# Weights prepared two chunks at a time, a bias table laid out in memory, and the product A12 B21 at the end of the last step: a neighbourhood-attention layer on one core

## The chip, the core and the metric

The kernel runs on one core of a Trainium2 chip. The metric is the device time of one execution in microseconds (us); of several runs the median is given. The engines are named as in the profile: PE (matrix products), DVE (vector), ACT (scalar), POOL (GpSimd), SP (issues DMAs).

## What is computed

One layer of the encoder, in float32, for x of 512 tokens (8 rows by 64 columns) by 2048:

```python
h = rms_norm(x, norm_pre)
q, k, v, z = jnp.split(h @ w_in, 4, axis=-1)            # w_in 2048 x 8192, 16 heads of 128
# one_row(r), for every row r of the grid; with 8 rows all 8 are keys, and 16 columns about the query's
s = jnp.einsum('bqhd,bxqyhd->bhqxy', q_r, k_nb) * scale
s = s + rpb[:, dr[None, :, None], dc[:, None, :]]
p = jax.nn.softmax(s over the 128 neighbours)
o = jnp.einsum('bhqxy,bxqyhd->bqhd', p, v_nb)
y = (o * jax.nn.silu(z)) @ w_out                        # w_out 2048 x 2048
return x + rms_norm(y, norm_post)
```

## The kernel before

**Products.** The big products go through PE in the format fp32r. Each operand is split into a high part `hi` (a cast on ACT) and the rest `lo` (a subtraction on DVE), and a product is hi·hi + lo·hi + hi·lo, three matmuls. Their results are accumulated in PSUM.

**Steps.** Work runs in ten steps over the columns of W, of 1024 columns each. Steps 0 to 7 multiply with W_in and give q, k, v, z of two heads each; steps 8 and 9 multiply with W_out. Steps 0 and 8 are plain: 32 chunks of 12 matmuls with 512 columns. The others use seven products in place of eight (Strassen's scheme in Winograd's form), of block sums of A (the activations: A11, S1, A12, N2, A22, N4, N3) and of B (the weights: B11, B12, B21, B22 and running sums of them): seven passes of 8 chunks, 6 matmuls a chunk. A *chunk* is 128 rows of W by 512 columns (256 KB). The passes accumulate in the chains X, Y, X, Y, Z, Y, Z of two PSUM banks each; `combine` takes a chain apart after each pass. m numbers all chunks in order: step 3 is m = 144 to 199, its pass 2 is 160 to 167, its pass 3 is 168 to 175.

**A chunk's way.** `load_raw` (L205) brings a raw chunk through SP's queue into one of four buffers (`NRAW`), `load_t` (L122) a chunk of B11 or B12 into one of eight tiles T. `prep(m)` (L216) runs two chunks (`AHEAD`) ahead of the matmuls of m: in passes 1, 3 and 4 it adds raw to T on DVE (L223), casts hi on ACT (L231) and subtracts lo on DVE (L232), each with three buffers; in pass 5 it adds raw to T after the split (L239). Then it issues the loads that became possible.

**Attention beside it.** Beside step s the attention of two heads of step s - 1 is computed, by the table `HEAD`: at a chunk number, for instance, transposes on PE (tk, tq, tz, L393; the copies k5h, k5l, q5h, q5l of head 5 are their split, L398 to L407), the scores (L457), the bias added with the row maximum (L470), exponentials, the transposition and split of p (pt, L504 and L405), the product with v (o, L527) and the gate (zm, L533). The PSUM buffers of tag T are two, so tz takes that of tk. The bias of a head comes as a padded table of 184 KB into `braw` (POOL's queue, L434); three operations on DVE reverse it and add a mask (L440).

**The last step.** In step 9, pass 6 is cut in halves of 128 tokens each (`products` with one half, L287): all chunks of half 0, then `combine_last(0)`, all of half 1, then `combine_last(1)`. `finish(n, t, ...)` squares a block of columns n for tokens t, sums, computes the factor rcy by a power on POOL (L657), and multiplies by the weights of the norm (L658). `final(t)` scales, adds the residual xres in four parts (three on DVE, L668, one on ACT and POOL, L665 and L666) and writes to memory. `load_res` (L672) brings xres from the middle of pass 4 on; `final(0)` and `final(1)` stand in pass 6.

**What sets the order.** Instructions are written in the order of the loop at the end, and the tile scheduler moves them within each engine, except those issued through `InOrder`. An engine takes its instructions strictly in the order that results, and waits for semaphores at the head of its queue.

Of the kernel before, what the change touches and what calls it, by code (L numbers as in the profile page):

```python
# [38 lines left out]

NSTEP = HEADS // 2  # L40
# [9 lines left out]
NRAW = 4  # L50
# [15 lines left out]
def na_block(ctx: ExitStack, tc: tile.TileContext, xT, x, gpre, gpost, w, rpb, mask, out):  # L66
# [29 lines left out]
    mhalf = cp.tile([P, 4], F32, name="mhalf")  # L96
    nc.gpsimd.memset(mhalf, -0.5)
    mask_sb = cp.tile([P, 3, 32], F32, name="mask_sb")
# [21 lines left out]
    T = [cp.tile([P, L], F32, name=f"t{k}") for k in range(KH)]  # L120

    def load_t(step, q, k):  # L122
        nc.sync.dma_start(T[k], w[step, q, k])

# [61 lines left out]
    def where(m):  # L186
# [5 lines left out]
        return step, *divmod(m, KT if step in PLAIN else KH)  # L192
# [12 lines left out]
    def load_raw(m):  # L205
        raws[m] = wp.tile([P, L], F32, tag="raw", name=f"raw{m}", bufs=NRAW)
        step, p, k = where(m)
        if step in PLAIN:
            src = w[step, (B11, B12, B21, B22)[p + 2 * (k // KH)], k % KH]
        else:  # L210
            src = w[step, (None, B12, B21, B22, B21, B22)[p], k]
        nc.sync.dma_start(raws[m], src)
# [3 lines left out]
    def prep(m):  # L216
        step, p, k = where(m)
        plain = step in PLAIN
        if step == 0 and p == 0:
            take_x(k)  # L220
        src = raws.pop(m) if is_raw(m) else T[k]
        if not plain and p in (1, 3, 4):
            nc.vector.tensor_tensor(T[k], T[k], src, ALU.add)  # L223
# [7 lines left out]
        nc.scalar.copy(hi, src)  # L231
        nc.vector.tensor_tensor(lo, src, hi.bitcast(F32), ALU.subtract)  # L232
# [5 lines left out]
        elif p == 5:  # L238
            nc.vector.tensor_tensor(T[k], T[k], src, ALU.add)  # L239
# [6 lines left out]
    U, C = {}, {}  # L246
# [33 lines left out]
    def mm_seven(m):  # L280
        step, p, k = where(m)
        c = chain(p)
        if p in (0, 1, 4) and k == 0:
            b = (step + (c == "Y")) % 2
            U[c] = [pm.tile([P, L], F32, tag=f"u{2 * b + s}", name=f"u{step}{c}{s}") for s in range(2)]
        if step == LAST and p == 6:
            products(m, (0,))  # L287
            if k == KH - 1:
                combine_last(0)
                for mm in range(m - KH + 1, m + 1):  # L290
                    products(mm, (1,))
                combine_last(1)
# [24 lines left out]
    def combine(step, p):  # L317
        u = U[chain(p)]
        c = C.setdefault(step, {})
        if p == 0:  # L320
            c["12"] = pair(f"s1_{step}")
            for s in range(2):
                nc.scalar.copy(c["12"][:, s, :], u[s])
        elif p == 1:
            c["21"] = pair(f"s5_{step}")
            for s in range(2):
                nc.scalar.copy(c["21"][:, s, :], u[s])
        elif p == 2:
            c["11"] = pair(f"c11_{step}")
            for s in range(2):  # L330
                if step == LAST:
                    finish(2, s, u[s], c["11"][:, s, :])
                else:
                    nc.scalar.activation(c["11"][:, s, :], u[s], AF.Copy, scale=rc[:, s : s + 1])
        elif p == 3:
            c["22"] = pair(f"e_{step}")
            for s in range(2):
                nc.vector.tensor_tensor(c["22"][:, s, :], u[s], c["12"][:, s, :], ALU.subtract)
            nc.vector.tensor_tensor(c["21"], c["22"], c["21"], ALU.subtract)
# [413 lines left out]
```

## Time and profile before

| | before |
|---|---|
| median of 3 runs | 910.19 us (908.84 to 910.43) |
| the profiled execution | 909.24 us, of which the span is 907.5 |
| granted PE clock, mean | 0.992 |
| DMA | 163.32 MB, mean 180 GB/s |
| ACT cast hi from T, 128x512 | 312 times, 618 ns |
| DVE bias and mask, 128x256 | 48 times, 603 ns |

The span is the stretch that the profile records. A row of the groups names line, engine, operation, tiles and shapes; behind the bar stand the busy time, the mean duration and the idle time of the engine just before, with what ended it. A window's row gives for each engine the busy time and (x) the instructions, then the granted PE clock (1.00 is full), the busy share of the DMA engines, and GB/s. Timeline rows begin with start and duration; an operation's duration can overlap its successor's on the same engine, so the distance between two starts is what one costs in a full queue.

### The profile page before, as it was taken

What the parts mean: (1) busy time and instruction counts of PE and PEld (TensorE: products, weight loads), DVE (VectorE), ACT (ScalarE), POOL (GpSimd) and SP (SyncE); (2) the same over time, 40 slices, a digit from 0 to 9 for tenths busy, and PEclk for the clock granted to TensorE, in tenths of its full rate; (3) what the DMA queues carried; (4) which work ended last, traced back from release to release, by engine and by line L of the source; (5) the groups of instructions that cost most, each with busy time, mean ns of one, the idle gap of its engine ahead of it and who ended that gap; (6) DMA issues with size and microseconds to landing.
All of it is one profiled execution on the core that took longest, in us unless ns stands there. A gap on an engine that the chain in (4) does not pass through costs nothing.

```text
span 907.5 us, 13123 instructions
## 1 busy us (share of the span) xinstructions
PE 879.1 (97%) x4184; PEld 729.6 (80%) x4184; DVE 756.4 (83%) x1395; ACT 563.0 (62%) x1077; POOL 36.2 (4%) x63
## 2 busy tenths in 40 slices
PE   9999999999999999999999999999999999999981
PEld 7888888888888888888888888888878888888660
DVE  4477979897988998799879987989799756886877
ACT  6666857585658566755776576758576654455342
POOL 1000000000000000000000000000002000000003
PEclk9999999999999999999999999999999999999996
DMA  8894367637664765476546745773676334544795
GB/s 258 247 266 129 94 183 220 194 101 217 211 173 114 232 203 165 123 233 199 148 148 214 223 140 159 219 209 116 185 255 192 106 117 127 153 137 147 237 219 185
DMA packets 85877, 163.32 MB, mean 180 GB/s; under 512 B 10016, under 2 KB 10016, under 8 KB 85808
## 3 DMA queue, kind: packets, MB, share of 16 engines
q1 hardware_dynamic: 82080, 151.56, 55.8%
q0 software_dynamic: 3296, 10.41, 4.4%
q8 instruction: 32, 0.52, 0.2%
q10 hardware_dynamic: 432, 0.53, 0.2%
q14 instruction: 37, 0.30, 0.1%
HBM read 154.59 MB, written 7.86 MB: 179 GB/s over the span
## 4 chain that ended last, share of the span: by engine, by line
PE 85%; issue 5%; DMA 4%; DVE 3%; POOL 1%; ACT 1%; SPq 0%; DVEq 0%; POOLq 0%; ACTq 0%
PE u L269 19%; PE u1Y L308 4%; PE u4Y L308 4%; PE u5Y L308 4%; PE u6Y L308 4%; PE u3Y L308 4%; PE u2Y L308 4%; DMA raw<-in_w 3%; PE u1X L308 2%; PE u4X L308 2%; PE u3X L308 2%; PE u2X L308 2%; PE u7X L308 2%; PE u5X L308 2%; PE u6X L308 2%
## 5 line engine op out<-in xcount | busy, mean ns | idle before, releaser
L231 ACT CAST hi<-t 128x512 fp32r<-128x512 f32 x312 | 192.0, 618 | 134.4 <-DVE lo L232 26.0
L232 DVE TENSOR_TENSOR lo<-t,hi 128x512 fp32r<-128x512 f32 x312 | 212.8, 688 | 29.8 <-ACT hi L231 29.0
L232 DVE TENSOR_TENSOR lo<-raw,hi 128x512 fp32r<-128x512 f32 x192 | 131.7, 690 | 66.0 <-ACT hi L231 53.2
L231 ACT CAST hi<-raw 128x512 fp32r<-128x512 f32 x192 | 118.7, 620 | 103.9 <-DVE lo L232 23.5
L223 DVE TENSOR_TENSOR t<-t,raw 128x512 f32<-128x512 f32 x192 | 128.4, 688 | 6.3 <-DMA raw<-in_w 5.7
L269 PE MATMUL u<-hi,a 128*128 128x512 f32 x512 | 131.1, 392 | 1.4 <-ACT a L145 0.8
L269 PEld LDWEIGHTS u<-hi,a 128*128 128x128 f32 x512 | 95.0, 188 | 21.5 <-ACT a L145 1.3
L269 PE MATMUL u<-lo,a 128*128 128x512 f32 x256 | 70.8, 390 | 0.0
L269 PEld LDWEIGHTS u<-lo,a 128*128 128x128 f32 x256 | 48.1, 188 | 10.1
L239 DVE TENSOR_TENSOR t<-t,raw 128x512 f32<-128x512 f32 x64 | 42.9, 689 | 7.7 <-DMA raw<-in_w 7.7
L308 PE MATMUL u9Y<-hi,a 128*128 128x512 f32 x96 | 27.0, 398 | 3.6 <-ACT hi L231 3.6
L440 DVE TENSOR_TENSOR bm<-braw,mask_sb 128x256 f32<-128x256 f32 x48 | 27.5, 603 | 0.0
L308 PE MATMUL u1Y<-hi,a 128*128 128x512 f32 x96 | 26.8, 396 | 0.0
L308 PE MATMUL u4Y<-hi,a 128*128 128x512 f32 x96 | 26.8, 396 | 0.0
L308 PE MATMUL u5Y<-hi,a 128*128 128x512 f32 x96 | 26.8, 396 | 0.0
L308 PE MATMUL u3Y<-hi,a 128*128 128x512 f32 x96 | 26.8, 396 | 0.0
L308 PE MATMUL u6Y<-hi,a 128*128 128x512 f32 x96 | 26.8, 396 | 0.0
L308 PE MATMUL u2Y<-hi,a 128*128 128x512 f32 x96 | 26.8, 396 | 0.0
L308 PE MATMUL u7Y<-hi,a 128*128 128x512 f32 x96 | 26.8, 396 | 0.0
L146 DVE TENSOR_TENSOR a<-x,a 128x512 fp32r<-128x512 f32 x16 | 11.0, 690 | 18.2 <-ACT a L145 18.2
L434 POOL DMA_DIRECT2D braw<-in_rpb x16 | 8.6, 535 | 436.1 <-DVE bm L440 252.0
L308 PEld LDWEIGHTS u9Y<-hi,a 128*128 128x128 f32 x96 | 17.6, 188 | 9.2 <-ACT hi L231 5.9
(444 smaller groups left out, 1958.0 us busy)
## 6 DMA issues: line engine op xcount, KB each, us to landing
raw<-in_w SPq DMA_DIRECT2D x384, 256.0 KB, 2.9
t<-in_w SPq DMA_DIRECT2D x128, 256.0 KB, 2.9
x<-in_xT SPq DMA_DIRECT2D x16, 256.0 KB, 5.5
xres<-in_x SPq DMA_DIRECT2D x16, 256.0 KB, 8.2
graw<-zm POOLq DMA_DIRECT2D x14, 256.0 KB, 3.6
out<-xres SPq DMA_DIRECT2D x14, 256.0 KB, 3.0
sq<-in_x SPq DMA_DIRECT2D x6, 512.0 KB, 9.2
braw<-in_rpb POOLq DMA_DIRECT2D x16, 184.0 KB, 3.9
```

The lines of the kernel that those rows point to most:

```text
L146: (vector or nc.vector).tensor_tensor(lo, src, hi.bitcast(F32), ALU.subtract)
L223: nc.vector.tensor_tensor(T[k], T[k], src, ALU.add)
L231: nc.scalar.copy(hi, src)
L232: nc.vector.tensor_tensor(lo, src, hi.bitcast(F32), ALU.subtract)
L239: nc.vector.tensor_tensor(T[k], T[k], src, ALU.add)
L269: nc.tensor.matmul(U[n][j], l, r, start=k == 0 and i == 0, stop=k == KT - 1 and i == 2)
L308: nc.tensor.matmul(U[c][s], l, r, start=p in (0, 1, 4) and k == 0 and n == 0, stop=k == KH - 1 and n == 2, skip_group_check=True,)
L434: nc.gpsimd.dma_start(raw[:, 0 : 7 * TBL + 32], src)
L440: nc.vector.tensor_tensor(bm[:, i, :].rearrange("p (a b) -> p a b", b=8), rev, mask_sb[:, i, :].unsqueeze(2).to_broadcast([P, 32, 8]), ALU ...
```

## The change

**Pairs.** Raw data, T, hi and lo are handled two chunks at a time: raw has two buffers of a pair (each loaded by a DMA of 512 KB), T four tiles of a pair, hi and lo two buffers of a pair each. Adds, casts and subtractions are 128x1024 (only the first four chunks are split one by one, and loaded x, raw, x, raw). `prep` runs once for two chunks. PSUM tiles of a chain are two banks in one tile, and `combine` works on both at once.

**Bias.** The host lays out the bias of each head with its mask as a table of 128 x 3 x 256; it is loaded as it is (393 KB a head), and the three DVE operations, the mask's load and `braw` are gone.

**The last step.** The passes run in the order `LATE = (0, 1, 3, 4, 5, 6, 2)`: the product of A12 and B21 comes last, cut in halves of tokens; its weights are prepared beside pass 6 into the tiles of N2 and A22. `finish` and the additions of `final` are all on DVE and stand in program order. xres comes earlier, from the second pass on, into tiles that are free by then, and `final(2)`, `final(3)` stand behind pass 6, `final(0)`, `final(1)` behind the halves.

```diff
-NRAW = 4
+LATE = (0, 1, 3, 4, 5, 6, 2)
+NRAW = 2
...
-        for n, ops in enumerate(((A11, N4, S1), (A12, A22), (N2, N3))):
+        for n, ops in enumerate(((A11,), (N4, S1), (A12, A22), (N2, N3))):
...
-    T = [cp.tile([P, L], F32, name=f"t{k}") for k in range(KH)]
+    T = [cp.tile([P, 2, L], F32, name=f"t{k}") for k in range(0, KH, 2)]
...
-        return step, *divmod(m, KT if step in PLAIN else KH)
+        p, k = divmod(m, KT if step in PLAIN else KH)
+        return step, LATE[p] if step == LAST else p, k
...
-    seq = [m for m in range(N) if is_raw(m)]
+    seq = [m for m in range(0, N, 2) if is_raw(m)]
     for i, m in enumerate(seq):
-        e = max(m - 6, seq[i - NRAW] if i >= NRAW else 0)
+        e = max(m - 6 if m < N - KH else 0, seq[i - NRAW] if i >= NRAW else 0)
...
-        raws[m] = wp.tile([P, L], F32, tag="raw", name=f"raw{m}", bufs=NRAW)
+        raws[m] = wp.tile([P, 2, L], F32, tag="raw", name=f"raw{m}", bufs=NRAW)
...
+            nc.sync.dma_start(raws[m], w[step, q, k : k + 2].rearrange("k p c -> p k c"))
...
-            nc.vector.tensor_tensor(T[k], T[k], src, ALU.add)
-            src = T[k]
...
+            nc.vector.tensor_tensor(T[k // 2], T[k // 2], src, ALU.add)
+            src = T[k // 2]
+        if m >= N - KH:
+            for i in range(2):
+                W[m + i] = hi, lo = [A(k + i, o).rearrange("p a b -> p (a b)") for o in (N2, A22)]
...
-            hi, lo = (wp.tile([P, L], F32R, tag=t, name=f"{t}{m}") for t in ("hi", "lo"))
+            hi, lo = (wp.tile([P, 2, L], F32R, tag=t, name=f"{t}{m}", bufs=2) for t in ("hi", "lo"))
...
+                U2[c] = pm.tile([P, 2, L], F32, tag=f"u{b}", name=f"u{step}{c}")
+                U[c] = [U2[c][:, s, :] for s in range(2)]
+        if m >= N - KH:
+
+            s, kk = divmod(2 * k, KH)
+            for j in (kk, kk + 1):
+                products(N - KH + j, (s,))
+            if kk + 2 == KH:
+                finish(2, s, U["X"][s], C[LAST]["11"][:, s, :])
+                final(s)
...
-        raw = sp.tile([P, L], F32, tag="braw", name=f"braw{h}")
...
-        bm_of[h] = (raw, sp.tile([P, 3, 256], F32, tag="bm", name=f"bm{h}"))
...
+        bm_of[h] = sp.tile([P, 3, 256], F32, tag="bm", name=f"bm{h}")
+        nc.gpsimd.dma_start(bm_of[h], rpb[h])
...
-            if q == 1:
-                nc.scalar.activation(yg[q, t], yg[q, t], AF.Copy, scale=rcy[:, col])
-                nc.gpsimd.tensor_tensor(r, yg[q, t], r, ALU.add)
-            else:
-                nc.vector.scalar_tensor_tensor(r, yg[q, t], rcy[:, col], r, ALU.mult, ALU.add)
+            dve.scalar_tensor_tensor(r, yg[q, t], rcy[:, col], r, ALU.mult, ALU.add)
...
-        at(base(LAST) + 4 * KH + 1 + 3 * k // 2, load_res, k)
-    for t in range(2):
-        at(base(LAST) + 6 * KH + t, final, t)
+        t, q = divmod(k, 4)
+        at(base(LAST) + KH + k, load_res, 2 + t, q)
+        at(base(LAST) + (5 * KH + 2 * q + 1 if t == 0 else 2 * KH + 2 * q), load_res, t, q)
+    for s in range(2):
+        at(base(LAST) + 6 * KH + 1 + s, final, 2 + s)
...
+        if m % 2 == 0 and N - 2 * KH <= m + AHEAD < N - KH:
+            prep(m + AHEAD + KH)
```

**The order on DVE in step 3, pass 3.** What stands there before, around the split of k of head 5 (k5l) and of q (q5l); t0 to t7 are the tiles T, the numbers of raw, hi and lo are chunks:

```order
L223 TENSOR_TENSOR t7_142<-t7_142,raw175_3257 128x512
L232 TENSOR_TENSOR lo171_3254<-t3_138,hi171_3253 128x512
L223 TENSOR_TENSOR t0_135<-t0_135,raw176_3270 128x512
L232 TENSOR_TENSOR lo172_3267<-t4_139,hi172_3266 128x512
L223 TENSOR_TENSOR t1_136<-t1_136,raw177_3289 128x512
L232 TENSOR_TENSOR lo173_3286<-t5_140,hi173_3285 128x512
L223 TENSOR_TENSOR t2_137<-t2_137,raw178_3311 128x512
L406 TENSOR_TENSOR k5l_3298<-tk5_3279,k5h_3297 128x512
L232 TENSOR_TENSOR lo174_3308<-t6_141,hi174_3307 128x512
L223 TENSOR_TENSOR t3_138<-t3_138,raw179_3333 128x512
L223 TENSOR_TENSOR t4_139<-t4_139,raw180_3358 128x512
L400 SCALAR_TENSOR_TENSOR q5l_3320<-tq5_3301,q5h_3319 128x512
```

And in the changed kernel, whose L236 is the add, L254 the subtraction of lo, L429 and L423 the splits:

```order
L254 TENSOR_TENSOR lo168_2628<-t0_140,hi168_2627 128x1024
L236 TENSOR_TENSOR t2_141<-t2_141,raw170_2603 128x1024
L236 TENSOR_TENSOR t4_142<-t4_142,raw172_2631 128x1024
L254 TENSOR_TENSOR lo170_2663<-t2_141,hi170_2662 128x1024
L545 SCALAR_TENSOR_TENSOR zm4_2426<-o4_2648,zm4_2426 128x512
L236 TENSOR_TENSOR t6_143<-t6_143,raw174_2666 128x1024
L254 TENSOR_TENSOR lo172_2683<-t4_142,hi172_2682 128x1024
L236 TENSOR_TENSOR t0_140<-t0_140,raw176_2686 128x1024
L429 TENSOR_TENSOR k5l_2707<-tk5_2695,k5h_2706 128x512
L254 TENSOR_TENSOR lo174_2717<-t6_143,hi174_2716 128x1024
L236 TENSOR_TENSOR t2_141<-t2_141,raw178_2720 128x1024
L423 SCALAR_TENSOR_TENSOR q5l_2729<-tq5_2710,q5h_2728 128x512
```

The splits keep their place among the chunks: k5l stands behind the add of chunk 178 before, and behind the add of the pair 176 and 177 now. Between k5l and q5l stood three operations of 512 columns, and now stand two of 1024.

**The order on PE in the product A12 B21 of the last step.** The end of its first half and the beginning of the second, with the semaphores on which they wait (u9X is the PSUM tile of the chain, a0_2 and the like hold A12 and A22 or the prepared weights):

```order
L336 MATMUL u9X_6886<-a6_2_134 128x512 [waits DVE_49]
L336 MATMUL u9X_6886<-a7_3_139,a7_2_138 128x512 [waits Activation_49]
L336 MATMUL u9X_6886<-a7_3_139,a7_2_138 128x512
L336 MATMUL u9X_6886<-a7_2_138 128x512 [waits DVE_49]
L336 MATMUL u9X_6886<-a0_3_111,a0_2_110 128x512 [waits DVE_49]
L336 MATMUL u9X_6886<-a0_3_111,a0_2_110 128x512
```

The second half begins on the fifth row, and has a wait on DVE: for the product of the first half's result with the norm's weights, which is read from the same PSUM tile. Before, pass 6 stood in this place, with a PSUM tile for each half.

**The order on DVE ahead of that product.** What stands there now (xres20 to xres33 are the residuals of `final(2)` and `final(3)`, c11 the result of the product's first half, line 64 is that of the helper that keeps the written order):

```order
L64 SCALAR_TENSOR_TENSOR xres20_6968<-y0_2_6553,cols_101,xres20_6968 128x512
L64 SCALAR_TENSOR_TENSOR xres21_6976<-y1_2_6869,cols_101,xres21_6976 128x512
L64 SCALAR_TENSOR_TENSOR xres22_6991<-s5_9_7045,cols_101,xres22_6991 128x512
L64 SCALAR_TENSOR_TENSOR xres23_6999<-e_9_7134,cols_101,xres23_6999 128x512
L64 SCALAR_TENSOR_TENSOR xres30_7014<-y0_3_6559,cols_101,xres30_7014 128x512
L64 SCALAR_TENSOR_TENSOR xres31_7022<-y1_3_6875,cols_101,xres31_7022 128x512
L64 SCALAR_TENSOR_TENSOR xres32_7037<-s5_9_7045,cols_101,xres32_7037 128x512
L64 SCALAR_TENSOR_TENSOR xres33_7047<-e_9_7134,cols_101,xres33_7047 128x512
L64 TENSOR_TENSOR c11_9_7389<-u9X_6886,gpost2_6501 128x512
```

And before, ahead of the blocks of pass 6 (s5 and e, the last that PE produced):

```order
L668 SCALAR_TENSOR_TENSOR xres2_8964<-y0_1_8084,rcy_146,xres2_8964 128x512
L668 SCALAR_TENSOR_TENSOR xres3_8981<-c11_9_8767,rcy_146,xres3_8981 128x512
L668 SCALAR_TENSOR_TENSOR xres3_8981<-s1_9_8559,rcy_146,xres3_8981 128x512
L362 TENSOR_TENSOR s5_9_8666<-u9Z0_8894,s5_9_8666 128x512
L363 TENSOR_TENSOR e_9_8882<-e_9_8882,u9Z0_8894 128x512
```

The result that the last product waits for stands behind the eight additions; before, the six additions of `final(0)` and `final(1)` on DVE stood ahead of the last results.

More of the change, by code (lines that the diff above doesn't have):

```diff
@@ L65, in na_block @@
 @with_exitstack
-def na_block(ctx: ExitStack, tc: tile.TileContext, xT, x, gpre, gpost, w, rpb, mask, out):
+def na_block(ctx: ExitStack, tc: tile.TileContext, xT, x, gpre, gpost, w, rpb, out):
     nc = tc.nc
@@ L95, in na_block @@
         nc.tensor.matmul(warm, ones, ones, start=True, stop=True)
-    mhalf = cp.tile([P, 4], F32, name="mhalf")
+    cols = cp.tile([P, 6, 4], F32, name="cols")
+    mhalf, rc, ms, ms3, msy, rcy = (cols[:, i, :] for i in range(6))
     nc.gpsimd.memset(mhalf, -0.5)
-    mask_sb = cp.tile([P, 3, 32], F32, name="mask_sb")
     edge = {}
@@ L243, in prep @@
             load_raw(r)
-    U, C = {}, {}
+    U, U2, C = {}, {}, {}
     def chain(p):
@@ L254, in mm_plain @@
             if n == 0:
-                U[n] = [pm.tile([P, L], F32, tag=f"u{j}", name=f"u{step}_0_{j}") for j in range(4)]
+                u = [pm.tile([P, 2, L], F32, tag=f"u{j}", name=f"u{step}_0_{j}") for j in range(2)]
+                U[n] = [u[j // 2][:, j % 2, :] for j in range(4)]
             else:
@@ L284, in mm_seven @@
             b = (step + (c == "Y")) % 2
[L285 to L292, printed above, removed]
+            if step == LAST and c == "Z":
+                U[c] = [px.tile([P, L], F32, tag="T", name=f"u{step}{c}{s}") for s in range(2)]
+            else:
+                U2[c] = pm.tile([P, 2, L], F32, tag=f"u{b}", name=f"u{step}{c}")
[7 more added lines that the diff above has]
+                final(s)
         else:
@@ L317, in combine @@
     def combine(step, p):
-        u = U[chain(p)]
+        u, u2 = U[chain(p)], U2.get(chain(p))
         c = C.setdefault(step, {})
+        tt = nc.vector.tensor_tensor
         if p == 0:
             c["12"] = pair(f"s1_{step}")
-            for s in range(2):
-                nc.scalar.copy(c["12"][:, s, :], u[s])
+            nc.scalar.copy(c["12"], u2)
         elif p == 1:
             c["21"] = pair(f"s5_{step}")
-            for s in range(2):
-                nc.scalar.copy(c["21"][:, s, :], u[s])
+            nc.scalar.copy(c["21"], u2)
         elif p == 2:
@@ L350, in combine @@
                     scale_c(c["12"], s, 0)
-        else:
-            for s in range(2):
-                nc.vector.tensor_tensor(c["21"][:, s, :], u[s], c["21"][:, s, :], ALU.subtract)
-                nc.vector.tensor_tensor(c["22"][:, s, :], c["22"][:, s, :], u[s], ALU.subtract)
+        elif step == LAST:
+            c["11"] = pair(f"c11_{step}")
+            for s in range(2):
+                dve.tensor_tensor(c["21"][:, s, :], u[s], c["21"][:, s, :], ALU.subtract)
+                dve.tensor_tensor(c["22"][:, s, :], c["22"][:, s, :], u[s], ALU.subtract)
+                finish(2, 2 + s, c["21"][:, s, :])
+                finish(3, 2 + s, c["22"][:, s, :])
+        else:
+            tt(c["21"], u2, c["21"], ALU.subtract)
+            tt(c["22"], c["22"], u2, ALU.subtract)
             for s in range(2):
@@ L463, in add_bias @@
         if a == 0:
-            col_of[h] = [sp.tile([P, 4], F32, tag=t, name=f"{t}{h}") for t in ("mx", "sm", "nm", "rs")]
+            t = sp.tile([P, 4, 4], F32, tag="col", name=f"col{h}")
+            col_of[h] = [t[:, i, :] for i in range(4)]
         mx, _, nm, _ = col_of[h]
@@ L595, in na_block @@
         at(when(h, 0) - (4 if late else 11), load_bias, h)
-        for i in range(3):
-            at(when(h, i) if late else when(h, 0) - 7 + i, bias, h, i)
     for pr in range(NSTEP):
@@ L608, in na_block @@
             at(early(h - 5), fetch_g, h)
-            at(early(h - 2), take_g, h)
+            at(early(h - 2), take, h)
         else:
-            at(when(h, 23), take_g, h)
+            at(when(h, 23), take, h)
     pending = {}
@@ L620, in na_block @@
         at(12 + 2 * i, lambda i=i: pending.pop(i)())
-    at(8, lambda: nc.gpsimd.dma_start(mask_sb, mask))
     at(28, rstd)
@@ L629, in na_block @@
             at(base(step) + KT + 2 * k, lambda k=k: split_a(k, X[k], N2, act, dve))
-            if step:
-                at(base(step) + KT + 2 * k, load_t, LAST, B11, k)
+            if step and k % 2:
+                at(base(step) + KT + 2 * k, load_t, LAST, B11, k - 1)
             at(base(step) + KT + 1 + 2 * k, lambda k=k: split_a(k, X[k + KH], N4, act, dve))
-    ms3 = cp.tile([P, 4], F32, name="ms3")
-    msy = cp.tile([P, 4], F32, name="msy")
-    rcy = cp.tile([P, 4], F32, name="rcy")
     yg, xres, gb = {}, {}, {}
@@ L741 @@
         "w": w,
-        "rpb": rpb,
-        "mask": _mask(),
+        "rpb": _bias(np.asarray(na_rpb)[0]),
     }
```

150 lines of the change are left out of this document (74 added, 76 removed).

## The prediction

> **What bounds the kernel now.** I read the page's first lines, then a table of windows cut at the steps' ends, then the waits of TensorE, then the timeline of one step. Span and busy shares:
>
> ```profile
> span 907.5 us, 13123 instructions
> PE 879.1 (97%) x4184; PEld 729.6 (80%) x4184; DVE 756.4 (83%) x1395; ACT 563.0 (62%) x1077; POOL 36.2 (4%) x63
> ```
>
> Windows (step 0 from 9.76, step 1, step 3, step 8, step 9 in three parts and the tail):
>
> ```profile
> core 0: us, PE busy (x) PEld busy (x) DVE busy (x) ACT busy (x) POOL busy (x), PEclk, DMA share, GB/s
> 9.76:94.42 84.66, 84.66 (x373) 70.14 (x374) 55.92 (x102) 56.65 (x99) 2.11 (x2) 1.00 0.78 217
> 94.42:181.47 87.05, 87.05 (x425) 72.84 (x425) 76.71 (x143) 56.33 (x111) 2.23 (x4) 1.00 0.61 177
> 268.41:355.21 86.80, 86.80 (x425) 72.76 (x425) 78.14 (x146) 57.10 (x111) 2.15 (x4) 1.00 0.60 180
> 702.50:802.78 100.28, 99.76 (x480) 82.64 (x479) 71.12 (x144) 55.31 (x115) 1.08 (x2) 1.00 0.42 129
> 802.78:826.00 23.22, 23.22 (x104) 19.22 (x104) 16.68 (x27) 13.94 (x26) 0.00 (x0) 1.00 0.30 95
> 826.00:850.00 24.00, 23.56 (x104) 19.18 (x103) 20.47 (x36) 10.46 (x20) 0.00 (x0) 1.00 0.68 211
> 850.00:875.00 25.00, 21.88 (x87) 15.15 (x86) 17.76 (x29) 9.46 (x16) 0.00 (x0) 1.00 0.99 262
> 875.00:907.50 32.50, 11.10 (x46) 7.99 (x45) 25.62 (x41) 9.75 (x22) 9.18 (x8) 0.78 0.63 180
> ```
>
> PE is busy without a gap in every step but the last, at a granted clock of 1.00, so there only fewer matmuls or a new wait can move the time. The change issues the same matmuls. From 94 to 702 us PE waits once:
>
> ```profile
> PE tz L393 <- DVE k13l L406: 0.9, 1, 0.9
> ```
>
> So steps 1 to 7 have nothing to gain and something to lose, and step 9 with its tail (104.7 us) has something to gain. What can be lost shows inside step 3 (passes 3, 4 and 5 lie in these rows):
>
> ```profile
> 302.00:314.70 12.70, 12.70 (x69) 10.77 (x68) 12.38 (x21) 6.91 (x13) 0.55 (x1) 1.00 0.82 256
> 314.70:326.00 11.30, 11.30 (x57) 9.57 (x56) 11.30 (x27) 7.79 (x19) 0.00 (x0) 1.00 0.59 189
> 326.00:338.00 12.00, 12.00 (x59) 9.92 (x58) 12.00 (x22) 7.87 (x17) 0.00 (x0) 1.00 0.75 230
> ```
>
> The step's mean says DVE has 8.7 us to spare (86.80 less 78.14); these rows say it has none from 302 to 338. What keeps PE fed there is the lead with which DVE enters: its first add of pass 3 is at 299.79, while PE begins that pass at 306.18.
>
> ```profile
> 299.79 0.69 DVE L223 TENSOR_TENSOR t<-t,raw 128x512 f32<-128x512 f32 x1
> 312.71 0.68 DVE L406 TENSOR_TENSOR k5l<-tk,k5h 128x512 fp32r<-128x512 f32 x1
> 315.11 0.69 DVE L400 SCALAR_TENSOR_TENSOR q5l<-tq,q5h 128x512 fp32r<-128x512 f32 x1
> 321.20 1.23 DVE L339 TENSOR_TENSOR s<-e,s 128x1024 f32<-128x1024 f32 x1
> 322.34 0.69 DVE L428 TENSOR_TENSOR zm<-tz,za 128x512 f32<-128x512 f32 x1
> 290.16 1.07 PE L308 MATMUL u3Y<-hi,a 128*128 128x512 f32 x4
> 306.18 1.09 PE L308 MATMUL u3Y<-hi,a 128*128 128x512 f32 x4
> 313.95 0.38 PE L393 MATMUL tz<-ident,s 128*128 128x128 f32 x2
> 316.01 0.28 PE L457 MATMUL s<-k5h,q5l 128*128 128x256 f32 x1
> ```
>
> k5l (whose end frees the PSUM buffer that tz of head 5 takes) ends at 313.39 and PE takes tz at 313.95: a margin of 0.56 us. q5l ends at 315.80 and the score that reads it starts at 316.01.
>
> **Steps 1 to 7: what DVE gains.** Durations of the operations that go or merge, and of the loads:
>
> ```profile
> L440 DVE TENSOR_TENSOR bm<-braw,mask_sb 128x256 f32<-128x256 f32 x6 | 3.5, 605 | 0.0
> L232 DVE TENSOR_TENSOR lo<-t,hi 128x512 fp32r<-128x512 f32 x40 | 27.3, 688 | 4.1 <-ACT hi L231 3.9
> L62 ACT ACTIVATE sq<-sq 128x1024 f32<-128x1024 f32 x8 | 8.5, 1056 | 0.0
> DMA to landing us min/median/max: 2.6/2.9/3.9
> ```
>
> The bias operations take 3.5 us of DVE per step, and go. Adds and subtractions merge in pairs: 44 a step (28 lo, 16 adds). A 128x512 lasts 0.69 us, but two in a row start 0.60 apart (299.79 and the rows like it), and the 1024-wide one starts 1.14 before its successor (321.20 to 322.34). A pair thus saves 1.20 - 1.14 = 0.06 us, 2.6 us a step; DVE goes to about 78.1 - 3.5 - 2.6 = 72.0. [...]
>
> **Steps 1 to 7: what DVE loses.** Its lead. Before, raw data has four buffers of a chunk and hi and lo three; now each has two buffers of a pair. A pair's cast must wait until PE has left the pair before the last, a load until the pair two ahead of it in raw has been read, and it lands later because it is twice as large: between 2.6 us plus 0.67 (262 KB at 393 GB/s, the best slice of the rows below) = 3.27, and 2.9 plus 1.02 (at 256 GB/s, the window from 302) = 3.92. I take 3.6, the middle, an estimate.
>
> Pass 2 of step 3: PE leaves pair 156 at about 290.2 (row at 290.16). Cast 160 takes 1.06 (the 1024-wide ACT row), lo 160 1.14: 292.4; raw 164 is issued and lands at 296.0. Cast and lo 164 to 298.3; raw 168 issued, lands at 302.0. Add 168, the first of pass 3, so starts 2.2 us later than 299.79. Ahead of k5l DVE's order then has eight pair operations (the adds 168, 170, 172, 174, 176 and lo 168, 170, 172) and two of 0.65: 8 x 1.14 + 2 x 0.65 = 10.4, and idle time for the cast of 168 (0.45) and for raws 172 and 174, each issued only after the add two before it (0.2 and 0.4): 302.0 + 11.5 = 313.5, k5l itself 0.69, and some 0.25 for hand-overs between the engines (my guess): its end comes at 314.45, before 313.39. PE wants tz at 313.95: a stall of 0.5. q5l now stands behind lo 174 and add 178: 314.45 + 2.28 + 0.69 = 317.4, against 316.01 + 0.5: with the two scores ahead of it, 0.7 more. The same lead lost is felt at k4l in pass 0 (0.3), at a lo of pass 4 (0.4) and of pass 5 (0.2), by the same count: **2.1 us a step, 14.7 in seven**. With 3.27 us for a load it is 1.1 a step (7.7), with 3.92 it is 2.9 (20). A stall lets DVE catch up, so 14.7 is nearer to the top of what these counts give than to their bottom. The bias load grows from 184 to 393 KB on POOL's queue, loaded 11 chunks ahead (15 us), so it is hidden; were it not, it would cost one landing.
>
> **Start and step 8.** The start loads the first four chunks interleaved as before; a mask load less, at most 0.9 us, I take 0.4 saved. Step 8 stalls 0.5 us and I leave it so (0 to 0.5 either way).
>
> **The last step.** Rows of its end and of its loads:
>
> ```profile
> xres<-in_x SPq DMA_DIRECT2D x15, 256.0 KB, 8.2
> raw<-in_w SPq DMA_DIRECT2D x9, 256.0 KB, 7.5
> GB/s 111 285 125 184 298 315 265 269 220 259 390 393 239 233 262 249 262 288 383 393 328 200 229 252 233 279 328 233 220 239 249 243 282 328 216 213 259 262 249 220
> 881.94 5.86 PE L308 MATMUL u9Z<-w,a 128*128 128x512 f32 x25
> 893.01 0.58 ACT L651 ACTIVATE ysq<-s 128x512 f32<-128x512 f32 x1
> 899.59 0.55 POOL L657 TENSOR_TENSOR rcy<-msy,mhalf 128x1 f32<-128x1 f32 x1 [2.08 <-DVE msy L656]
> 900.17 0.75 DVE L668 SCALAR_TENSOR_TENSOR xres<-y,rcy,xres 128x512 f32<-128x512 f32 x1 [0.66 <-POOL rcy L657]
> 901.51 1.75 DVE L668 SCALAR_TENSOR_TENSOR xres<-e,rcy,xres 128x512 f32<-128x512 f32 x1
> ```
>
> Before: 336 matmuls of 0.227 us (48 in 10.9) are 76.2 us, but PE ends at 887.80, 85.0 after the start, because loads saturate the queue (DMA share 0.99): 8.8 us of waiting; then 19.7 us of tail. After: six whole passes (65.3) and stalls. (a) Pass 1 is followed by pass 3, on the same chain Y, so PE waits for one 1024-wide copy behind a cast, 2 x 1.06 = 2.1. (b) The loads of xres move up into the second and third pass: 12 of them with 16 chunks are 28 x 262 KB = 7.3 MB, 28.0 us at 262 GB/s against 21.8 of matmuls; two pairs are ahead, so I take half of the 6.2, 3.1. (c) Small waits of pair preparation, 2.2, one step's worth. That puts the end of pass 6 at 65.3 + 7.4 = 72.7. Then the first half of A12 B21, 24 x 0.227 = 5.4, to 78.1. The second half waits: its PSUM tile is one with the first's, and DVE's product of the first half stands behind 22 operations that begin at 72.7, among them the eight additions of finals 2 and 3: 8 x 0.65 + 8 x 0.67 + 6 x 0.13 and 0.65 for itself = 12.0, to 84.7. So 6.6 us of stall where the matmuls were to close up. Second half to 90.1; then square 0.8, product 0.65, msy 0.2, power 0.66, four additions 2.75 (no POOL addition beside them, so 0.67 to 0.75 instead of 1.75), and 4.25 from the last addition to the end of the span (903.26 to 907.5): 99.4, against 104.7. **Gain 5.3**, from 2 (all 6.2 of (b)) to 8 (no (b)).
>
> **The sum**, on the profiled execution (909.24 us, span 907.5): 909.24 + 14.7 - 5.3 - 0.4 = 918.2. The median of the runs is 0.95 above that execution: 919.2.
>
> **Rivals.**
> 1. No new stall in steps 1 to 7: the 6.1 us freed on DVE per step give back the lead, and the change is faster. For it: DVE idles while it waits for casts in pass 2, and the margin that fails is only 0.56 us. Against: the lead is set by buffers and landings. It decides if raw 168 lands before 301.5. Price: 909.24 - 5.3 - 0.4 + 0.95 = 904.5. Chance 0.30.
> 2. Loads land in 3.27 us, with half the stalls: 7 x 1.1 = 7.7 in place of 14.7, that is 912.2. Chance 0.15. [...]
> 3. The early loads of xres cost their whole 6.2 us: 919.2 + 3.1 = 922.3, and with loads at 3.92 more. Chance 0.10.
> 4. The pair tile does not hold the second half back (the change then does what it says): 6.6 less, 912.6; the second half's first matmul has that semaphore wait, so the chance is 0.05, counted within the forecast's.
>
> **Numbers.** The forecast itself has 0.45 (rival 4 included). About 0.2% (1.8 us) can be told from no change. Faster is rival 1 but for its upper end, 0.28; within 0.2% (908.4 to 912.0) lie that end, 0.02, and the lower part of rival 2, 0.06; the rest is slower, 0.64. The range runs from 903 (rival 1 with a better last step) to 925 (rival 3); the likeliest case's own is 911 to 924.
>
> **What would show it.** In each of steps 1 to 7 PE rows waiting on DVE k, q or lo operations of 0.2 to 0.7 us, a step of about 89 us; raw landings near 3.6 us; in the last step a wait of about 6 us of u9X on a DVE product, and no addition over 0.8 us at the end. Steps of 86.8 us as before would prove the main term wrong; a last step as long as before would prove the gain wrong.

## The result, and the profile after

The changed kernel takes 924.76 us (924.26 to 926.32, 4 runs) against 909.52 us before: the ratio is 1.0171, with an interval of 1.0152 to 1.0189. It is slower, as forecast, but by 15.2 us where 9.0 were forecast. On the scale of the 910.19 us that the prediction started from, 1.0171 is 925.8 us, just above the range's upper end of 925. On another chip the same kernel was slower by less: 919.61 us against 908.88 (ratio 1.0105, 1.0080 to 1.0131), and 920.44 against 909.30 in a second set there. So part of the loss differs from one chip to the next. (Of two kernels below a single execution took about twice as long, 1800 and 1984 us, and medians and comparisons leave it out.)

The page of the changed kernel, its span, its engines and its raw loads:

```profile
span 923.2 us, 11462 instructions
PE 890.2 (96%) x4184; PEld 730.7 (79%) x4184; DVE 704.1 (76%) x952; ACT 518.8 (56%) x823; POOL 29.2 (3%) x58
raw<-in_w SPq DMA_DIRECT2D x190, 512.0 KB, 3.5
```

PE has as many instructions as before and is busy longer. The first matmuls of steps 1, 8 and 9 in the timeline of PE, after:

```profile
94.14 0.39 PE L336 MATMUL u1X<-hi,a 128*128 128x512 f32 x1
720.33 0.39 PE L292 MATMUL u<-hi,a 128*128 128x512 f32 x1
819.84 0.39 PE L336 MATMUL u9X<-hi,a 128*128 128x512 f32 x1
```

and before:

```profile
94.26 0.39 PE L308 MATMUL u1X<-hi,a 128*128 128x512 f32 x1
703.75 0.39 PE L269 MATMUL u<-hi,a 128*128 128x512 f32 x1
802.62 0.39 PE L308 MATMUL u9X<-hi,a 128*128 128x512 f32 x1
```

From these starts and the two spans comes the whole account:

| part | before | after | difference | forecast |
|---|---|---|---|---|
| to the start of step 1 | 94.26 | 94.14 | -0.12 | -0.4 |
| steps 1 to 7 | 609.49 | 626.19 | +16.70 | +14.7 |
| step 8 | 98.87 | 99.51 | +0.64 | 0 |
| step 9 to the end of the span | 104.88 | 103.36 | -1.52 | -5.3 |
| span | 907.5 | 923.2 | +15.7 | +9.0 |

PE's waits after, the longest of them:

```profile
PE u9X L336 <- DVE c L64: 6.6, 1, 6.6
PE u9Y L336 <- ACT s L354: 1.8, 1, 1.8
PE tz L416 <- DVE k13l L429: 1.1, 1, 1.1
PE tz L416 <- DVE k7l L429: 0.8, 1, 0.8
PE u2Y L336 <- DVE lo L254: 0.8, 1, 0.8
PE s L468 <- DVE q13l L423: 0.7, 1, 0.7
PE u3Y L336 <- DVE lo L254: 0.7, 1, 0.7
PE s L468 <- DVE q5l L423: 0.5, 1, 0.5
```

Where before stood one row of 0.9 us for steps 1 to 7, there is now a list: tz of one head waits for its k, a score for its q, a product for its lo. The rows don't add up to the 2.4 us by which a step grew, since the list leaves out small gaps that several matmuls in a row have.

The windows of step 3, of the last step up to the end of the last product's first half, of a stretch within that, of the wait, of the second half in two parts, and of the tail:

```profile
core 0: us, PE busy (x) PEld busy (x) DVE busy (x) ACT busy (x) POOL busy (x), PEclk, DMA share, GB/s
272.73:362.29 89.56, 88.14 (x425) 72.52 (x424) 71.77 (x91) 52.39 (x81) 2.18 (x4) 1.00 0.55 179
819.84:899.00 79.16, 74.50 (x313) 58.98 (x311) 63.12 (x74) 35.29 (x50) 0.56 (x1) 0.98 0.66 199
845.50:849.25 3.75, 3.75 (x11) 2.88 (x10) 3.18 (x3) 1.05 (x1) 0.00 (x0) 0.54 0.86 270
899.00:905.50 6.50, 0.00 (x0) 0.00 (x0) 6.50 (x12) 0.69 (x2) 0.98 (x1) 0.86 0.57 175
905.50:909.50 4.00, 3.92 (x9) 3.15 (x10) 2.88 (x6) 0.00 (x0) 0.54 (x1) 0.50 0.96 311
909.50:913.70 4.20, 4.12 (x16) 2.97 (x14) 0.00 (x0) 0.04 (x1) 0.00 (x0) 0.88 0.56 182
913.70:923.20 9.50, 0.00 (x0) 0.00 (x0) 3.55 (x6) 0.64 (x2) 0.54 (x1) 0.69 0.36 110
```

In step 3 DVE has less to do, 71.77 us, and the step is longer. In the last product's second half the column PEclk reads 0.50 and 0.88, that is, half the clock until about 910.5: its 24 matmuls take 8.0 us (905.58 to 913.62) and not 5.4. And there is an earlier such stretch, which the mean of 0.98 hides: about 3.4 us at half the clock from 845.7 on, right behind PE's wait for the copy:

```profile
843.58 1.20 PE L336 MATMUL u9Y<-hi,a 128*128 128x512 f32 x4 [1.82 <-ACT s L354]
```

Step 3 again, the DVE rows of pass 3 that answer to those of the prediction:

```profile
306.58 1.23 DVE L236 TENSOR_TENSOR t<-t,raw 128x1024 f32<-128x1024 f32 x1 [1.01 <-DMA raw<-in_w]
314.73 1.22 DVE L236 TENSOR_TENSOR t<-t,raw 128x1024 f32<-128x1024 f32 x1 [0.34 <-DMA raw<-in_w]
317.01 1.22 DVE L236 TENSOR_TENSOR t<-t,raw 128x1024 f32<-128x1024 f32 x1
318.14 0.68 DVE L429 TENSOR_TENSOR k5l<-tk,k5h 128x512 fp32r<-128x512 f32 x1
321.12 0.68 DVE L423 SCALAR_TENSOR_TENSOR q5l<-tq,q5h 128x512 fp32r<-128x512 f32 x1
```

Step 3 starts 4.49 us later than before. Less that, the first add is at 302.09 (forecast 302.0), k5l ends at 314.33 (forecast 314.45), q5l at 317.31 (forecast 317.4). The brackets name what the adds waited for: raw data.

### The profile page after: what moved, and what is told of

The parts are those of the page before. It is cut to its first block, busy times and chain, and to the rows that moved or that the text cites. A ratio compares the mean times of both kernels' runs of the same rounds, so it can differ in the third digit from the quotient of the medians.

```text
span 923.2 us, 11462 instructions
## 1 busy us (share of the span) xinstructions
PE 890.2 (96%) x4184; PEld 730.7 (79%) x4184; DVE 704.1 (76%) x952; ACT 518.8 (56%) x823; POOL 29.2 (3%) x58
## 4 chain that ended last, share of the span: by engine, by line
PE 50%; DMA 21%; DVE 18%; issue 5%; ACT 5%; SPq 0%; DVEq 0%; POOLq 0%; ACTq 0%; POOL 0%
DMA raw<-in_w 19%; PE u L292 15%; DVE lo L254 8%; DVE t L236 4%; ACT hi L253 3%; PE u5Y L336 3%; PE u5Z L336 2%; PE u1Y L336 2%; PE u4Y L336 2%; PE u6Y L336 2%; PE u3Y L336 2%; PE u2Y L336 2%; PE s L468 2%; DMA x<-in_xT 1%; PE o L539 1%
## 5 line engine op out<-in xcount | busy, mean ns | idle before, releaser
L253 ACT CAST hi<-t 128x1024 fp32r<-128x1024 f32 x160 | 167.8, 1050 | 166.5 <-DVE t L236 30.7
L254 DVE TENSOR_TENSOR lo<-t,hi 128x1024 fp32r<-128x1024 f32 x160 | 195.3, 1221 | 45.5 <-ACT hi L253 44.4
L254 DVE TENSOR_TENSOR lo<-raw,hi 128x1024 fp32r<-128x1024 f32 (+1 forms) x94 | 112.7, 1200 | 72.3 <-ACT hi L253 72.2
L253 ACT CAST hi<-raw 128x1024 fp32r<-128x1024 f32 (+1 forms) x94 | 96.8, 1030 | 76.9 <-DMA raw<-in_w 41.5
L236 DVE TENSOR_TENSOR t<-t,raw 128x1024 f32<-128x1024 f32 x96 | 117.2, 1223 | 23.0 <-DMA raw<-in_w 22.0
L261 DVE TENSOR_TENSOR t<-t,raw 128x1024 f32<-128x1024 f32 x32 | 39.1, 1223 | 13.9 <-DMA raw<-in_w 13.1
L392 ACT ACTIVATE s<-s,cols 128x512 f32<-128x512 f32 x28 | 18.7, 717 | 7.0 <-DVE s L384 4.4
L428 ACT CAST pt_1h<-pt 128x512 fp32r<-128x512 f32 x16 | 9.4, 587 | 20.6 <-PE pt L516 20.6
L147 DVE TENSOR_TENSOR a<-x,a 128x256 fp32r<-128x256 f32 (+1 forms) x24 | 11.4, 510 | 12.2 <-ACT a L146 12.2
```

What stands on the lines that cost most here:

```text
L236: nc.vector.tensor_tensor(T[k // 2], T[k // 2], src, ALU.add)
L253: nc.scalar.copy(hi[:, i, :], src[:, i, :])
L254: nc.vector.tensor_tensor(lo[:, i, :], src[:, i, :], hi[:, i, :].bitcast(F32), ALU.subtract)
L261: nc.vector.tensor_tensor(T[k // 2], T[k // 2], src, ALU.add)
L392: nc.scalar.activation(t[:, s, :], t[:, s, :], AF.Copy, scale=rc[:, j + s : j + s + 1])
L428: nc.scalar.copy(hi, t)
```

## The experiments

The theory was that steps 1 to 7 stall because raw data has lost its lead. The first rival was that it comes of the coarser pieces on DVE and of the two pair buffers of hi and lo. The kernels of experiments 1 to 4 ran on one chip, another than the first, and the kernel before took 908.31 us there. "Step" means below the time from the first matmul of step 1 to that of step 8, divided by seven. In the two profiles above it is 87.07 us before and 89.46 in the changed kernel. On the chip of experiments 1 to 4 the measure for the changed kernel's steps is experiment 4, whose edit lies behind them: 88.56.

**1. Raw data in chunks again.**

```diff
-NRAW = 2
+NRAW = 4
...
-        raws[m] = wp.tile([P, 2, L], F32, tag="raw", name=f"raw{m}", bufs=NRAW)
+        raws[m] = wp.tile([P, L], F32, tag="raw", name=f"raw{m}", bufs=NRAW)
...
+            for i in range(2):
+                t = T[k // 2][:, i, :]
+                nc.vector.tensor_tensor(t, t, src[i], ALU.add)
```

> The changed kernel with its raw data in four buffers of one chunk again (loads of 256 KB, adds to T of 512 columns, casts straight from raw of 512 columns); hi and lo stay two buffers of a pair. Theory (the stalls of steps 1 to 7 are lost lead of raw data: a buffer is freed later and filled 0.6 us later): most of the 16.6 us that these steps and the one before step 8 have grown by goes, steps of 86.9 to 87.5 us, 909 to 912 us in all. Rival (the stalls come of coarse operations on DVE, 1.14 us ahead of short urgent ones, and of hi and lo in two buffers of a pair): steps stay above 88.5 us, 920 to 925.

908.8 us, ratio 1.0010 (0.9995 to 1.0026): as fast as before. The step is 87.48 us, 1.1 less than with pairs (88.56). The waits of PE in steps 1 to 7, then the landing of its raw loads there:

```profile
PE s L475 <- DVE q7l L430: 0.7, 1, 0.7
PE s L475 <- DVE q13l L430: 0.5, 1, 0.5
PE s L475 <- DVE q9l L430: 0.2, 1, 0.2
```

```profile
DMA to landing us min/median/max: 2.5/2.9/5.9
```

The stalls on tz and on lo are gone, with hi and lo still in two pairs. A remainder may be the rival's: q in some steps, 0.4 us a step against the 87.07 of the first chip.

**2. Hi and lo in chunks, raw in two pairs.**

```diff
-            hi, lo = (wp.tile([P, 2, L], F32R, tag=t, name=f"{t}{m}", bufs=2) for t in ("hi", "lo"))
+            W[m] = hi, lo = [wp.tile([P, L], F32R, tag=t, name=f"{t}{m}") for t in ("hi", "lo")]
...
+            nc.scalar.copy(hi, src[:, m % 2, :])
+            nc.vector.tensor_tensor(lo, src[:, m % 2, :], hi.bitcast(F32), ALU.subtract)
```

> The changed kernel with hi and lo in three buffers of one chunk each and casts and subtractions of 512 columns, as before; raw data stays two buffers of a pair, with adds of 1024 columns. Theory (lead of raw): the stalls stay or grow, since a raw buffer that is cast directly is freed one chunk later: 923 to 930 us, steps of 89 us or more. Rival (coarse operations and the two buffers of hi and lo): steps of 87 us, 909 to 912.

917.6 us, ratio 1.0120 (1.0087 to 1.0154), a step of 88.20 us. That meets neither forecast: 923 or more was the theory's, 912 or less the rival's. Most of the loss stays, and the readers of raw (over steps 1 to 7) still idle for its loads:

```profile
its engine sat idle before it (us, times) until:
  DMA raw<-in_w: 52.0, 58
```

The finer pieces, or what comes with them in this edit (a third buffer of hi and lo, and some loads issued a chunk earlier), do take something off the 88.56 of pairs.

**3. The same with three pairs of raw.** `NRAW = 3` in the kernel of experiment 2.

> As the kernel with hi and lo by chunks, and with three buffers of a pair for raw (the space that hi and lo give back). Theory (lead of raw): the stalls go, steps of 86.8 to 87.3 us, 908 to 911 us in all, with the changed last step kept. Rival (coarse operations, two buffers of hi and lo): no difference to the kernel with two buffers of raw.

906.81 us, ratio 0.9974 (0.9957 to 0.9991), a step of 87.28. One buffer is the only difference to experiment 2, and 10.8 us go with it between the medians. The profiled executions differ by 7.8 us of span (912.8 to 905.0), of which 6.4 lie in steps 1 to 7. In steps 1 to 7 PE has one wait, with loads that land as late as the changed kernel's on the first chip (3.4 us in both), and step 3 is dense:

```profile
PE u5Y L343 <- DVE lo L255: 0.2, 1, 0.2
```

```profile
DMA to landing us min/median/max: 3.1/3.4/6.6
```

```profile
267.21:354.29 87.08, 87.08 (x426) 72.75 (x424) 74.15 (x119) 56.94 (x109) 2.18 (x4) 1.00 0.55 185
```

So 512 KB a load does no harm by itself. The harm is two buffers with it.

**4. The finals behind the first half.**

```diff
-        at(base(LAST) + 6 * KH + 1 + s, final, 2 + s)
+        at(base(LAST) + 6 * KH + 4 + s, final, 2 + s)
```

> The changed kernel with final(2) and final(3) written behind the first half of the last product instead of ahead of it, nothing else. Theory (PE's 6.6 us wait is for DVE to come through the eight additions, and the lower granted clock after it follows from that wait): the wait shrinks to about 1.6 us, the second half runs at clock 1.00 in 5.4 us instead of 8.1, DVE is then the bound of the end: last step 98 us instead of 103.4, 918 to 921 us in all. Rival (the clock falls at this place for another reason, or the end is bound by DVE anyway): wait gone, second half still 8 us, or the span not more than 2 us shorter, 922 to 924.

914.19 us, ratio 1.0074 (1.0045 to 1.0103), better than either forecast, in part because steps 1 to 7 lose less on this chip (88.56 a step). The last step is what was to be tested: 98.4 us (812.62 to the span's 911.0), forecast 98. The first matmul of the second half, and the window of that half:

```profile
893.03 0.73 PE L336 MATMUL u9X<-a,a 128*128 128x512 f32 x2 [1.56 <-DVE c L64]
```

```profile
893.00:900.00 7.00, 5.73 (x24) 4.43 (x24) 6.35 (x11) 0.69 (x2) 0.54 (x1) 1.00 0.57 172
```

The wait is 1.56 us, and the 24 matmuls take 5.7 us at a clock of 1.00. It is shown that the wait was for DVE's eight additions. That the clock fell because PE idled is not shown by this, since DVE's work was moved too.

**5. The changed kernel again**, on the chip of kernels 5 to 10 (before: 908.88 us).

> The changed kernel as it is, on the chip of these runs, as the measure for the others. Theory and rival alike: 920 to 926 us, the 6.6 us wait of the last product there, and the stalls of steps 1 to 7 as long as the raw loads take to land on this chip (2.0 to 2.5 us a step at 3.5 us, less at 3.3).

919.61 us, ratio 1.0105 (1.0080 to 1.0131), a step of 88.95, the last step 103.4. So this execution differs from the first chip's in steps 1 to 7 (3.5 us) and at the start (1.2 us), and not in the last step. Raw loads land in 3.3 us here, 3.4 on the first chip (median of steps 1 to 7).

**6. The bias table alone**, in the kernel before.

```diff
-        bm_of[h] = (raw, sp.tile([P, 3, 256], F32, tag="bm", name=f"bm{h}"))
+        bm_of[h] = sp.tile([P, 3, 256], F32, tag="bm", name=f"bm{h}")
+        nc.gpsimd.dma_start(bm_of[h], rpb[h])
```

> The kernel before with the bias table alone: the 48 operations on DVE are gone, raw data, hi and lo and the last step stay. Theory (with PE dense in steps 1 to 7, room on DVE is worth nothing but the one wait of 0.9 us in step 7): 0 to 2 us less than before. Rival (DVE's 27 us bound the kernel in places that the waits don't show): 4 us less or more.

907.5 us against 908.88, ratio 0.9986 (0.9971 to 1.0001), as the theory has it. Its last step, whose code is that of before, lasts 102.9 us here, where the profile of before has 104.9. DVE has 75.42 us of work in step 3 (it was 78.14), and that step takes the 86.8 us it took:

```profile
268.90:355.66 86.76, 86.76 (x425) 72.72 (x424) 75.42 (x140) 56.92 (x111) 2.18 (x4) 1.00 0.60 185
```

**7. The residuals later.**

```diff
-        at(base(LAST) + KH + k, load_res, 2 + t, q)
+        at(base(LAST) + 4 * KH + k, load_res, 2 + t, q)
```

> The changed kernel with the eight loads of the residuals of final(2) and final(3) three passes later (beside the fifth pass of the last step instead of the second). Theory (these loads hold back raw data in the second and third pass): the waits for lo and hi between 25 and 58 us of the last step, 5.6 us in the first profile, fall by 2 to 4 us, and the kernel gains as much, since nothing else is loaded beside the pass of sums. Rival (those waits come of the pair buffers alone): unchanged within 1 us, or new waits later of the same size.

918.2 us (917.78 to 918.64) beside 919.61 (915.97 to 920.24) for the changed kernel: within its spread. The last step is 102.6 us instead of 103.4. Its two long waits up to the last product are now:

```profile
PE u9Z L336 <- ACT hi L253: 2.0, 1, 2.0
PE u9Y L336 <- ACT s L354: 1.8, 1, 1.8
```

On the same chip the unchanged order had 4.9 us of waits for lo ahead of that. They are gone, so the early loads did cause them; but a wait of 2.0 us and one of 0.3 stand later. Beside them PE's matmuls start 0.43 us apart from 881.05 to about 884.0, where they start 0.23 apart before and behind; so they do in the first profile at the clock of 0.50. The last product's second half takes 8.4 us, where it took 7.5 on this chip. The theory's place was right and its gain was not.

**8. Both repairs.** The kernel of experiment 3 with the line of experiment 4.

> hi and lo by chunks with three buffers, raw in three pairs, and the two finals behind the first half of the last product. Theory: the two repairs add up, since one acts in steps 1 to 7 and the other at the end: 3 to 5 us less than the first of them alone, 901 to 904 us, faster than the kernel before by 0.5 to 0.8%. Rival (the end is bound by DVE, and the waits of the last step move): no more than 2 us from the second repair, 905 to 907.

902.33 us (900.25 to 904.66), ratio 0.9928 (0.9910 to 0.9946): faster than both kernels of this case, 0.7% under the one before. The last step with its tail is 98.4 us again, where the profile of before has 104.9, and 102.9 was seen with before's code on this chip (experiment 6).

**9 and 11. The wait filled.**

```diff
+                if s == 0:
+                    fill = px.tile([P, L], F32, tag="T", name="fill")
+                    for i in range(27):
+                        nc.tensor.matmul(fill, A(0, p)[:, 0, 0:P], W[N - KH][0], start=True, stop=True)
```

> The changed kernel with 27 matmuls of 128x512 (6.1 us, into a PSUM tile that nobody reads) between the two halves of the last product, where PE waits 6.6 us for DVE. Nothing is left out and nothing else moves. Theory (the granted clock falls to 0.50 because PE stood idle, and costs the second half 2.6 us): the wait that is left is under 1 us, the second half runs at clock 1.00 in 5.4 to 5.8 us instead of 8.1, and the span is 2 to 3 us shorter than the changed kernel's on the same chip, although PE has more to do. Rival (the clock falls at this place by its work so far or by the loads and stores beside it): second half 8 us again, span the same.

917.2 us in the median, ratio 1.0091 (1.0065 to 1.0117). The trace that is read here was taken on another chip:

> The kernel with the filled wait once more, for a profile at full clock: the first one's was of an execution in which PE ran at half speed from end to end (1984 us; the six other runs 914 to 918). Theory (the clock falls to 0.50 because PE stood idle): less than 1 us of wait ahead of the second half, that half at clock 1.00 in 5.4 to 5.8 us. Rival (another reason at this place): 8 us.

916.28 us, ratio 1.0091 (1.0059 to 1.0123). The last product's first matmul of the second half, and the windows of the filling and of that half:

```profile
896.99 0.74 PE L340 MATMUL u9X<-a,a 128*128 128x512 f32 x2 [0.31 <-DVE c L64]
```

```profile
890.40:896.99 6.59, 6.28 (x28) 4.88 (x26) 6.59 (x12) 0.69 (x2) 0.98 (x1) 1.00 0.55 156
896.99:902.75 5.76, 5.73 (x24) 4.43 (x24) 2.81 (x5) 0.00 (x0) 0.54 (x1) 1.00 0.98 317
```

DVE is as busy as it was, the same wait for c ends it, and DMA is at 0.98 during the half: in this place nothing has changed but that PE had something to do, and the clock stays at 1.00. The second half takes 5.7 us. So it is shown that PE's idle stretch lowers the clock here. It cost 2.3 us beyond its own length in the first profile. In experiments 5, 7 and 10, with such a wait (6.4 to 6.5 us), the half takes 7.1 to 8.4 us, which is 1.4 to 2.6 us over 5.7. In experiments 1, 2 and 3 (waits of 6.1 to 6.6 us) the longest matmul of the last product lasts 0.79 to 0.80 us, as in the first profile (0.80); with the wait filled it lasts 0.50.

**10. The changed kernel a second time** on the chip of experiments 5 to 9.

> The changed kernel as it is, the measure for the filled wait on the same chip. 916 to 926 us; the wait of 6.6 us and a second half of 8 us; steps 1 to 7 the longer, the longer raw loads take to land (88.9 us a step at a median of 3.3 us, 89.4 at 3.4).

920.44 us (913.89 to 922.05), ratio 1.0111 (1.0062 to 1.0160). The filled wait's median is a good 3 us below that. The second half is 7.1 us here, so the clock explains 1.4 of it in the profiled execution; the rest lies within a spread of 8 us.

## Why the prediction was off

**What bounds the kernel, and the lead.** Right in mechanism and nearly in size. The times of the events in step 3 came within 0.15 us; the 0.25 us for hand-overs between the engines in them was the author's guess, and no run shows it by itself. Experiments 1 and 3 each give raw data its lead back in another way (smaller buffers freed sooner, one buffer more), and each takes most of the stalls away, the one with hi and lo in pairs, the other with adds of 1024 columns. So the stalls go with either of these two left in place, and the lead of raw data is what the two have in common. What the readers of raw waited for shows in the view of its tiles from 94 to 700 us, after:

```profile
its engine sat idle before it (us, times) until:
  DMA raw<-in_w: 47.6, 60
...
DMA to landing us min/median/max: 3.2/3.4/7.2
```

and before:

```profile
its engine sat idle before it (us, times) until:
  ACT hi L231: 27.7, 51
...
DMA to landing us min/median/max: 2.5/2.8/5.4
```

Before, the readers of raw waited mostly for the cast ahead of them in their own chain, and 8.0 us for loads; after, 44.1 us for casts and 47.6 for loads.

**Steps 1 to 7, +14.7 forecast, +16.7 measured.** By the first matmuls of the passes, after less before, in the mean of the seven steps: pass 3, put at 1.2 us (tz and q), cost 1.2; pass 0, put at 0.3, cost 0.15; pass 4, put at 0.4, cost 0.6; pass 5, put at 0.2 for a lo, cost 0.44, with 0.7 to 0.8 us of waiting in steps 2 and 3 (u2Y and u3Y in the waits). So the terms of passes 4 and 5 were too small. Pass 5 reads a raw buffer twice, for the split and for the add to T, and frees it only behind the second; that this is the reason is argued and was not tried by itself. On the chip of experiment 5 the seven steps cost 13.2 us more than the 609.49 of before's profile.

**DVE's gain.** 72.0 us a step forecast, 71.77 measured in step 3. It was worth nothing that can be told from noise for the bias (experiment 6); the wider adds were not tried by themselves. Back to back, a 1024-wide operation starts 1.13 us ahead of its successor (317.01 to 318.14), so the 0.06 us that the rows gave for a pair stands.

**Landing of a pair.** 3.6 us taken, 3.4 to 3.5 measured, with 3.27 as the lower bound and 3.1 to 3.2 the shortest seen. In the traces of the kernels with pairs of raw the median of steps 1 to 7 lies 0.2 to 0.3 above the shortest.

**Start, step 8.** 0.4 us was forecast for the start and 0.1 came; step 8 grew by 0.64 us, which had been left at nothing: its first wait, on DVE, went from 0.5 to 0.9 us.

**The last step, -5.3 forecast, -1.5 measured. Here the prediction failed.** Its chain of waits held: the copy's stall was put at 2.1 us and is 1.8; the early residuals and the pairs together at 5.3, and what PE lost besides before the end of pass 6 is 4.9; the wait of the second half at 6.6, and it is 6.6; the tail after PE at 9.3, and it is 9.6. The step that failed is the price of a matmul behind such a wait. "Second half to 90.1" took 5.4 us for 24 matmuls, 0.227 us each as at the clock of 1.00; they ran at 0.50 for about 5 us and took 8.0. In the same way the "65.3" of the six whole passes has no room for the 3.4 us at half the clock behind the copy's stall, which cost 1.7, so that the first half ended 1.0 us later than put, at 79.1 us of the step. No term of the sum stood for the clock.

The profile of before could have warned of it. PE waits there in step 9 for at most 1.1 us at a time, and the clock stays at 1.00; but PE's last matmul ends at 887.80, and these windows behind it show the clock falling to 0.50, by the 0.81 some 5.3 us later:

```profile
887.80:890.00 2.20, 0.00 (x0) 0.00 (x0) 2.20 (x3) 0.00 (x0) 0.73 (x1) 1.00 0.83 250
890.00:895.00 5.00, 0.00 (x0) 0.00 (x0) 4.93 (x12) 1.97 (x7) 0.55 (x1) 0.81 0.92 311
895.00:900.00 5.00, 0.00 (x0) 0.00 (x0) 4.51 (x8) 1.31 (x3) 2.15 (x2) 0.50 0.44 122
```

The 0.78 of the prediction's own last window is this fall. A wait that was put at 6.6 us is longer than 5.3. In each of the seven traces with a wait of 6.1 us or more the matmuls behind it were slow (0.79 us or more for the longest, or 0.43 us from start to start, in place of 0.23), and with the same gap filled they were not. The fall itself came 4.7 us after the last matmul in the changed kernel's wait, 3.7 us behind PE's last matmul there, and 5.3 us in before; in some executions matmuls were slow behind waits of 1.8 to 2.5 us too. That the short waits cause it is argued from their place and was not tried. With the 2.6 us of the second half the time would have been put at 921.8, with the 1.7 as well at 923.5.

How much of the 1.5 us gained belongs to the change is open: before's code took 102.9 us for this step in experiment 6 and 104.9 in the first profile, the changed kernel 103.4 to 103.6 in three.

**The range.** On the second chip the ratio of 1.0105 is 919.7 us on the prediction's scale, close to the forecast, and that is luck: the last step took 103.4 us there too, where 99.4 was put. The range's upper end was set by residual loads and slow landings, and not by a difference between chips. The kernel before differs by about 1 us between the chips of this study, the changed one by 5. It hangs on the landing of a load in each of its steps, but that the 0.1 us between the chips' median landings is the cause is not shown.

**The rivals.** No new stall (904.5) was wrong for this kernel. With one buffer more (experiment 3) it nearly holds for steps 1 to 7, but the kernel is 1.5 us faster than before and not 5.7: by the profiles its last step gains 4.1 us (104.88 to 100.78), and steps 1 to 8 lose 2.7. With the finals moved too (experiment 8) it is 6.6 faster. Rival 2's landing was too short on the first chip; on that of experiment 5 loads landed in 3.3 us, nearly its 3.27, and the steps still cost 13.2 us and not 7.7, so its price for them was too low. Rival 3 put 6.2 us on the early loads of xres, and the waits before the end of pass 6 leave no room for that. Rival 4 came about only when the finals were moved (experiment 4).

## What to carry to other kernels

Doubling a load's size while halving its buffers keeps the bytes and loses the lead (here 16.7 us in steps 1 to 7): count how long before its use a buffer is free and filled, and not how busy an engine is on average. An engine that has no gap cannot be sped up by lightening its helpers (2.7 us less for DVE in step 3 left the step at 86.8 us in experiment 6). And a wait of PE that lowers its clock costs more than its length (6.6 us, and 2.3 more in the first profile): move other work behind the one result that the next matmuls wait for, or keep PE busy meanwhile. Read the clock in windows of a few microseconds, since a step's mean hides such a stretch (0.98 over 79.16 us, with 3.4 us at 0.50 in it).

## What the runs showed of the hardware

In seven traces (the first profile and experiments 1, 2, 3, 5, 7 and 10) PE waits 6.1 to 6.6 us within the last product. In the first profile the granted clock fell to 0.50 at 903.7, 4.7 us after the last matmul ahead of the wait, and stayed there for 6.8 us, which reached 4.9 us into the matmuls that followed. These started 0.43 us apart at the clock of 0.50 and 0.23 apart at 1.00. By that distance the slow stretch reached 2.9 us into them in experiment 10, 3.9 in 5 and some 5.6 in 7. In experiments 1 to 3 the longest of them lasted 0.79 to 0.80 us, as in the first profile. With a wait of 1.56 us (experiments 4 and 8), or with the wait filled (experiment 11), they started 0.23 us apart, at a clock of 1.00 in the windows of 4 and 11.

Behind PE's last matmul of all the clock fell to 0.50 as well, 3.7 us after it in the changed kernel (at 917.3) and 5.3 us after it in the kernel before (at 893.1).

At the end of PE's waits of 1.86, 1.98 and 2.45 us in the last step (experiments 4, 7 and 10), or up to 1.8 us after it, the matmuls started 0.43 us apart for 3.0 to 3.5 us. Soon after the copy's wait of 1.8 us the clock was at 0.50 in the first profile, from 845.7 to 849.1; in experiments 4, 5, 7, 10 and 11 the matmuls right behind that wait started 0.23 us apart.

In steps 1 to 7 a load of 512 KB landed in 3.1 to 3.2 us at the shortest and 3.3 to 3.4 in the median of a trace (the first profile and experiments 2 to 5 and 7), where one of 256 KB took 2.4 to 2.5, and 2.8 to 2.9 (before, experiments 1 and 6).
